# Retention's gate as seven half-size products between the value blocks, and the first head's projection between retention's steps

## The chip, the cores and the metric

The kernel runs on one core of a Trainium2 chip. Its engines run side by side, each with an instruction stream of its own, and wait for each other through semaphores: TensorE (PE) multiplies into the PSUM banks, VectorE (DVE) and ScalarE (ACT) take the results out and prepare operands, GpSimd (POOL) does small elementwise work, and SP, ACT and POOL issue the DMAs. An engine takes its instructions strictly in order; what stands behind a waiting instruction waits with it. The metric is the device time of one execution in microseconds (us): the median of the runs before is 1484.71 us, from 1483.43 to 1484.89.

## What is computed

One step of a decoder layer for a prompt of 1024 tokens and 8 single decode tokens: a mixer (differential attention beside retention), attention into a memory, and an MLP. The change concerns the input projection of the mixer and retention. Cut to that:

```python
z = rmsnorm(x) @ w_in                    # 1024 features in
qa, ka, va, qr, kr, vr, gr = split(z)    # va, vr and gr: 512 columns each
# retention, 4 heads, chunks of 128 tokens (C)
scores = (q @ k.T) * decay
o      = scores @ v + (q @ S) * exp((i + 1) * lg)
S      = exp(C * lg) * S + k_dec.T @ v
r      = head_rms(o) * silu(gr)          # gr is the gate
x      = x + concat(a, r) @ w_out        # a: attention, from qa, ka, va
```

Matrix products run in a reduced-precision fp32 form. So each operand is split into a high part and a low rest (names ending in h and l, or UH/UL and wh/wl), and a product takes three matmuls: high by high, high by low, low by high.

## The kernel before

Five stretches follow each other on TensorE at the front of the kernel, and the change touches all but the first.

1. **Projection of retention's q and k** for all tokens, while x is loaded.
2. **Value block "va"** and **value block "vr"**, both by `token_block` (L478). A block computes a projection of 512 columns for 1024 tokens as seven products of half-size matrices in place of eight (a Strassen-like scheme: the right operands are quadrants of the weights or their sums, the left ones quadrants of x or their sums in `XT`). The seven products come in the order 1, 2, 6, 7, 4, 5, 3, with 48 matmuls of 256 columns each, 336 in all, and 32 more with few rows for the decode tokens. Their results are added up by ACT and DVE in the tiles `va` or `vr`, in SBUF (L530 to L540). `between` hangs work of the other engines between the products: `after_va` writes the finished va rows to DRAM by DMAs that ACT issues (L594), rotates some q/k rows (`rotate`, on POOL and DVE) and makes bias rows; `after_vr` rotates the others and fetches and splits the gate's weights.
3. **Retention's 8 steps** (loop over `t`), one per 128 tokens. A step transposes q and k (`tr`, to `qblk` on ACT and `kT` on DVE), multiplies the scores `sc`, masks them into `Sm` (DVE), forms the state's increment `st` and the output `op` from `Sm`, v and the running state `S`. Between these short pieces stands the gate's projection for the same 128 tokens as filler, `grp` (`tokproj_parts`, L405): 24 matmuls of 512 columns per step, dealt out by `SEG = (3, 4, 0)` groups of three. At t = 2 come 16 more matmuls for the decode tokens' gate. The end of a step is `head_norm_gate`: squares of `op` on ACT (`jk`), a small scaling on DVE (`s4`), a power on POOL (`r4`), and the multiplication by the gate on DVE. One step later `to_operand` transposes the result (`trR`), splits it (`rh` on ACT, `rl` on DVE), and POOL issues two DMAs that write it to DRAM (`OPH`, `OPL`).
4. **Attention's first head**: `head_proj(0)`, 144 matmuls of 344 columns named `qkp`. The first 36 and then as many as complete two thirds of it, 96 in all, run as a block; then come 36 more (`START`) while `load_part` splits the keys (`KA`, `KB`), which POOL's DMAs copy into place on other partitions.
5. **Attention's score loop**, beginning with the matmuls `sp<-KA,Q`, whose gaps the rest of the projections fills.

The order on each engine is written out in the code: a `pin` keeps the matmuls in program order, `behind(...)` puts instructions after the last one of another engine, and the rest follows the order of the code by a scheduler. The number of buffers of a tile (`bufs`) sets when its next use may begin.

Of the kernel before, what the change touches and what calls it, by code (L numbers as in the profile page):

```python
# [10 lines left out]
F32 = mybir.dt.float32  # L11
# [3 lines left out]
ALU = mybir.AluOpType  # L15
# [33 lines left out]
def decoder_step(ctx: ExitStack, tc: tile.TileContext, i: dict, o: dict):  # L49
# [113 lines left out]
    ord_ = dram.tile([4, 8, P], F32, tag="ord", name="ord_")  # L163

# [17 lines left out]
    t_front, v_front = ExitStack(), ExitStack()  # L182
# [203 lines left out]
    with pool("a") as A:  # L386
# [6 lines left out]
        def decproj(units, name, PS, out, bufs=3):  # L393

            ps = PS.tile([P, 512], F32, tag="acc", name=name, bufs=bufs)

            dproj(ps, units)
            merge_parts(ps, out, name)
            return out

# [3 lines left out]

        def tokproj_parts(units, t, name, PS):  # L405
            ps = PS.tile([P, 512], F32, tag="acc", name=name, bufs=3)
            tk = slice(t * P, t * P + P)
            for kt in KT_PAIRS:
                w = [u[:, (kt // 4) * 512 : (kt // 4) * 512 + 512] for u in units[kt % 4]]
                mm(ps, UH[:, kt, tk], w[0], kt == 0, False)  # L410
                mm(ps, UH[:, kt, tk], w[1], False, False)
                mm(ps, UL[:, kt, tk], w[0], False, kt == 7)
                yield ps
# [64 lines left out]
        def token_block(ready, nm, out_dec, fetch, between, after):  # L478
# [12 lines left out]
            def scale(t):  # L491
                if t > 3 and nm == "vr":
                    return
                y = acc[t // 2][:, t % 2, :]
                cs = slice(256, 512) if t < 4 else slice(0, 512)
                nc.scalar.activation(y[:, cs], y[:, cs], AF.Copy, scale=rstd1[:, t : t + 1])

            order = (1, 2, 6, 7, 4, 5, 3)
            for n, q in enumerate(order):
# [13 lines left out]
                for pb in range(2):  # L513
# [14 lines left out]
                    with behind("Activation", "DVE"):  # L528
                        if q == 1:
                            nc.scalar.copy(lo[:, :, b], pv)  # L530
                        elif q == 2:
                            for j in range(2):
                                nc.scalar.activation(lo[:, j, a], pv[:, j, :], AF.Copy, scale=rstd1[:, 2 * pb + j : 2 * pb + j + 1])
# [7 lines left out]
                if q in (1, 2, 4, 5):  # L541
# [6 lines left out]
                    if q == 5:  # L548
                        merge_parts(psd, out_dec, nm)
                        nc.scalar.activation(out_dec, out_dec, AF.Copy, scale=rstd1[:8, 8:9])  # L550
# [35 lines left out]
        rot_va, rot_vr = {4: 8, 5: 0, 3: 1}, {1: 2, 2: 3, 6: 4, 7: 5, 4: 6, 5: 7}  # L586

        def after_va(q, acc):
# [8 lines left out]
            if q in rot_va:  # L597
                rotate(rot_va[q])

        def after_vr(q, acc):  # L600
            if q in rot_vr:
                rotate(rot_vr[q])
            if q == 5:
                nc.scalar.dma_start(vrd, vr8[:8])
                nc.scalar.activation(silu, half, AF.Silu)
            if q in (5, 3):
                for u in range(2):
                    if q == 3:
                        late = G.tile([P, T], F32, tag="raw", name="raw_g1", bufs=3) if u else G.tile([P, T], F32, tag="rb2", name="raw_g0")
                        nc.sync.dma_start(late[:, :1024], i["wall"][U_TOK + 10 + u])  # L610
                        late_raws.append(late)
                    else:
                        units.append(unit(U_TOK + 8 + u))
# [12 lines left out]
        units, late_raws = [], []  # L626
        pin[0] = True
        op_vr = token_operands(U_TOK + 4, "vr")
        token_block(op_va, "va", vdec[:8], rot_va, after_va, op_vr)
        vr8 = A.tile([P, 512], F32, tag="t1", name="vr_8", bufs=1)  # L630
        vacc = token_block(op_vr, "vr", vr8[:8], rot_vr, after_vr, lambda q: None)
# [3 lines left out]
        t_front.close()  # L635
        r_front = ExitStack()
        A = r_front.enter_context(pool("r", side="right"))
# [14 lines left out]
        def head_norm_gate(src, gate, n, t, out):  # L652
# [3 lines left out]
            for h in range(4):  # L656
                jk = A.tile([P, P], F32, tag="jk", name=f"jk_{t}_{h}")
# [8 lines left out]
        def to_operand(src, n, t, tag, tags=("rh", "rl", 1)):  # L666

            tr = PS.tile([P, 512], F32, tag="tr", name=f"trR_{tag}", bufs=tags[2])
# [13 lines left out]
        gate_d = A.tile([8, 512], F32, tag="gate_d", name="gate_d")  # L682

        tr = PS.tile([P, 512], F32, tag="acc", name="tr_d", bufs=3)
# [6 lines left out]
        def decode_step(p):  # L691
            so = raw_tile(A, f"so_{p}")
# [21 lines left out]

        S = None
        uqk = {}
        pend = None
        pin[0] = True
        for t in range(8):
            tr = PS.tile([P, 512], F32, tag="tr", name=f"tr_{t}", bufs=1)  # L720
# [8 lines left out]
            if t == 6:  # L729
                with behind("DVE"):  # L730
                    next(scaled)
            grp = tokproj_parts(units, t, f"grp_{t}", PS)
            for _ in range(SEG[0]):
                next(grp)
# [3 lines left out]
            Sm = A.tile([P, 512], F32, tag="Sm", name=f"Sm_{t}", bufs=2)  # L738
            nc.vector.tensor_mul(Sm, sc, maskM)
            if t == 0:  # L740
                with behind("Activation", "DVE"):
                    units += [unit(U_TOK + 10 + u, raw=late_raws[u]) for u in range(2)]
# [4 lines left out]
            if pend:  # L747
                pend()
            for _ in range(SEG[1]):
                next(grp)  # L750
            if t == 3:
                with behind("SP"):
                    nc.sync.dma_start(brep, bass.AP(tensor=brow[:, :].tensor, offset=brow[:, :].offset, ap=[[0, P], [1, 4 * BIASW]]))
            if t == 7:
                uqk[0] = [unit(U_QK + x) for x in range(2)]
# [13 lines left out]
            S = Sn  # L769
# [1927 lines left out]
```

## Time and profile before

One execution was profiled. Its own time is 1483.49 us, 1.2 us below the median of the runs.

| what | value |
|---|---|
| time of the profiled execution | 1483.49 us |
| span of its instructions | 1481.7 us |
| granted TensorE clock, mean | 0.997 of full |
| ACT busy, share of the span | 46% |
| POOL busy, share of the span | 21% |
| DMA, mean over the span | 160 GB/s |

The page gives for each engine the time in which an instruction ran and its share of the span. Matmuls overlap each other in their pipeline, so the duration of one (say 0.28 us) is longer than the distance at which the next one starts (0.118 us); distances between starts give the cost of a matmul in a row of them. Rows of a group or a tile show a count, durations (least, median, most, or the mean) and when the first and the last one started. Rows of waits show who waited for whom, in total, how often, and the longest wait.

### The profile page before, as it was taken

The numbers are of one execution on the slowest core, as the hardware profiler recorded it, in microseconds if no ns is written. First come the engines' busy times: TensorE is split into PE (matmuls) and PEld (weight loads), VectorE is DVE, ScalarE is ACT, GpSimd is POOL, SyncE is SP. The second block draws the span as 40 slices with busy tenths as digits, with TensorE's granted clock in tenths as the row PEclk, the third lists the DMA queues.
The fourth block names the chain that finished last, engine by engine and source line by source line (L and its number), as shares of the span: only waits on it lengthen the run. The fifth ranks groups of instructions, "written<-read, shape, count | busy, mean of one in ns | idle before, by whom it ended". The sixth has DMA issues, their size and how long they took to land.

```text
span 1481.7 us, 27906 instructions
## 1 busy us (share of the span) xinstructions
PE 1468.0 (99%) x10917; PEld 1399.2 (94%) x10917; DVE 1097.3 (74%) x2265; ACT 677.6 (46%) x1328; POOL 305.6 (21%) x331
## 2 busy tenths in 40 slices
PE   9999999999999999999999999999999999999998
PEld 7899779999679999989999999999999999999998
DVE  7666536888768545567877987888888888787876
ACT  6534435666552341258536544333434443343454
POOL 0035333122214311106022000000001311110380
PEclk9999999999999999999999999999999999999998
DMA  8255738214846177474582443334446774536273
GB/s 288 68 187 169 205 70 190 72 34 143 253 145 242 68 247 189 118 237 109 179 299 69 157 148 131 141 137 157 158 144 211 239 252 143 172 102 194 79 130 115
DMA packets 125784, 236.69 MB, mean 160 GB/s; under 512 B 13654, under 2 KB 75787, under 8 KB 125524
## 3 DMA queue, kind: packets, MB, share of 16 engines
q1 hardware_dynamic: 90826, 174.52, 37.2%
q0 software_dynamic: 23632, 40.60, 10.2%
q10 hardware_dynamic: 11194, 19.78, 3.6%
q8 instruction: 86, 1.41, 0.4%
q14 instruction: 46, 0.38, 0.1%
HBM read 170.24 MB, written 57.52 MB: 154 GB/s over the span
## 4 chain that ended last, share of the span: by engine, by line
PE 90%; DVE 5%; ACT 2%; issue 1%; DMA 1%; ACTq 0%; POOL 0%; SPq 0%; DVEq 0%
PE dn L2345 21%; PE Z L2177 9%; PE qkp L75 7%; PE pr_o L75 6%; PE mq L75 6%; PE pr_m L75 6%; PE X L2177 6%; PE Y L2177 6%; PE grp L75 3%; PE sp L75 2%; PE av L75 2%; PE mv L75 2%; PE mk L75 1%; PE mpv L75 1%; PE vap_z L522 1%
## 5 line engine op out<-in xcount | busy, mean ns | idle before, releaser
L2345 PE MATMUL dn<-UH,wd 128*128 128x258 f32 (+1 forms) x1800 | 325.9, 283 | 0.9 <-DVE c L2479 0.8
L2345 PEld LDWEIGHTS dn<-UH,wd 128*128 128x128 f32 x1800 | 278.7, 189 | 1.8 <-DVE c L2479 0.8
L2345 PE MATMUL dn<-UL,wd 128*128 128x258 f32 x900 | 253.9, 282 | 0.0
L2345 PEld LDWEIGHTS dn<-UL,wd 128*128 128x128 f32 x900 | 169.7, 189 | 0.1
L2479 DVE TENSOR_TENSOR c<-c,dn 128x258 f32<-128x258 f32 (+1 forms) x217 | 88.8, 417 | 36.7 <-PE dn L2345 34.2
L2203 ACT ACTIVATE hq<-r 128x258 f32<-128x258 f32 x128 | 53.7, 421 | 118.0 <-DVE r L2202 117.9
L2177 PE MATMUL Z<-T_h,wu 128*128 128x258 f32 x512 | 98.1, 283 | 0.0
L2177 PE MATMUL X<-UH,wu 128*128 128x258 f32 x512 | 97.5, 282 | 0.0
L2321 ACT CAST wd<-raw_d 128x512 fp32r<-128x512 f32 x96 | 58.7, 619 | 79.6 <-PE dn L2345 74.1
L1985 ACT CAST wu<-raw_up 128x512 fp32r<-128x512 f32 x96 | 59.0, 616 | 61.0 <-PE Z L2177 53.2
L2314 ACT CAST UH<-raw_h 128x1032 fp32r<-128x1032 f32 x56 | 58.7, 1055 | 53.3 <-PE dn L2345 27.7
L2177 PEld LDWEIGHTS X<-UH,wu 128*128 128x128 f32 x512 | 81.3, 188 | 0.0
L2177 PEld LDWEIGHTS Z<-T_h,wu 128*128 128x128 f32 x512 | 81.3, 189 | 0.0
L2315 DVE TENSOR_TENSOR UL<-raw_h,UH 128x1032 fp32r<-128x1032 f32 x56 | 73.7, 1315 | 8.4 <-ACT UH L2314 8.4
L2322 DVE TENSOR_TENSOR wd<-raw_d,wd 128x512 fp32r<-128x512 f32 x96 | 72.2, 758 | 10.3 <-ACT wd L2321 10.3
L2214 POOL DMA_DIRECT2D HT<-ht x32 | 17.1, 536 | 292.0 <-DVE ht L2213 271.6
L2177 PE MATMUL Z<-T_l,wu 128*128 128x258 f32 x256 | 72.3, 282 | 0.0
L2177 PE MATMUL X<-UL,wu 128*128 128x258 f32 x256 | 72.3, 282 | 0.0
L128 ACT CAST wh_u<-raw_u 128x1024 fp32r<-128x1024 f32 x43 | 44.5, 1048 | 57.3 <-PE mq L75 36.4
L1986 DVE TENSOR_TENSOR wu<-raw_up,wu 128x512 fp32r<-128x512 f32 x96 | 64.8, 689 | 3.7 <-ACT wu L1985 3.7
L129 DVE TENSOR_TENSOR wl_u<-raw_u,wh_u 128x1024 fp32r<-128x1024 f32 x39 | 48.6, 1257 | 19.8 <-ACT wh_u L128 19.6
L75 PE MATMUL qkp<-UH,wh_u 128*128 128x344 f32 x192 | 62.8, 327 | 0.1
(606 smaller groups left out, 4657.2 us busy)
## 6 DMA issues: line engine op xcount, KB each, us to landing
raw_u<-in_wall SPq DMA_DIRECT2D x49, 512.0 KB
HT<-ht POOLq DMA_DIRECT2D x32, 516.0 KB, 3.0
raw_h<-HT SPq DMA_DIRECT2D x32, 516.0 KB
raw_up<-in_wall SPq DMA_DIRECT2D x32, 512.0 KB
raw_d<-in_wall SPq DMA_DIRECT2D x32, 512.0 KB
HQ<-hq ACTq DMA_DIRECT2D x32, 387.0 KB
raw_h<-HQ SPq DMA_DIRECT2D x24, 516.0 KB
cmk<-in_cmk SPq DMA_DIRECT2D x16, 512.0 KB
```

Source lines behind the costliest of these rows:

```text
L75: pinned(nc.tensor.matmul(out, l, r, start=start, stop=stop))
L129: (lo_engine or nc.vector).tensor_sub(wl[:, :n], raw[:, :n], wh[:, :n].bitcast(F32))
L1985: nc.scalar.copy(w[:, :512], src)
L1986: nc.vector.tensor_sub(w[:, 512:], src, w[:, :512].bitcast(F32))
L2177: pinned(nc.tensor.matmul(ps, l, r[:, k, :], start=first and k == 0 and x == 0, stop=k == 3 and x == 2, skip_group_check=True))
L2203: nc.scalar.activation(h[:, PLACE[quad], :], r, AF.Square)
L2314: nc.scalar.copy(h, rv)
L2315: nc.vector.tensor_sub(l, rv, h.bitcast(F32))
L2321: nc.scalar.copy(w[:, :512], src)
L2322: nc.vector.tensor_sub(w[:, 512:], src, w[:, :512].bitcast(F32))
L2345: pinned(nc.tensor.matmul(ps[:, part], l, r[:, k, cq], start=first and k == 0 and x == 0, stop=k == 3 and x == 2, skip_group_check=True))
L2479: nc.vector.tensor_add(y, y, ps)
```

## The change

- **The gate becomes a third block "ga"** of `token_block` between "va" and "vr", with Silu as the function that takes the results out of PSUM. `grp`, its 16 decode matmuls and `SEG` are gone. The gate's weights are laid out like those of the values.
- **The gate's rows go through DRAM.** ACT issues eight DMAs of 256 KB and a small one into the new tensor `gated`; retention's steps fetch their rows back on SP's queue (`fetch_gate`).
- **Work between the products moves.** The rotations of `after_vr` move to `after_ga`; the load of the Silu table and a one-column Silu, which stood in the vr block's product 5, move to the end of va. The 2304 KB copy `brep`, from retention's step 3, is issued in the vr block's product 1; `rb`, a broadcast row that attention needs, in its product 3; the split of head 0's weights (`head_units(0)`) in its product 5.
- **`head_proj(0)` fills retention's steps**, by `RFILL = (8, 6, 5)`: 8 matmuls ahead of the loop, then 6 between `st` and `op` and 5 after `op`, 96 in all. The transposes of the next step (`turn_step`) move between `st` and `op`, the multiplication by the gate moves into the next step, `trR` comes after `op`, and head 1's weights are split in step 5.
- **After the loop** come `load_stacks` and `load_part` at once, 30 matmuls of filler, the last `to_operand`, and 6 more (`START = 6`).
- **Buffers**: `acc` banks 3 to 2, `tr` 1 to 2, `Sm` 2 to 1, the gate's tiles 2 to 3.

The core of the diff:

```diff
-        def tokproj_parts(units, t, name, PS):
-            ps = PS.tile([P, 512], F32, tag="acc", name=name, bufs=3)
...
+            if q == 3:
+                nc.scalar.activation(silu, half, AF.Silu)
+
+        def after_ga(q, acc):
+            if q in rot_ga:
+                rotate(rot_ga[q])
+            for t in {5: range(4), 3: range(4, 8)}.get(q, ()):
+                nc.scalar.dma_start(gated[t * P : t * P + P, :], acc[t // 2][:, t % 2, :])
+            if q == 5:
+                nc.scalar.dma_start(gated[NT:, :], ga8[:8])
 
         def after_vr(q, acc):
-            if q in rot_vr:
-                rotate(rot_vr[q])
+            if q == 1:
+                nc.sync.dma_start(brep, bass.AP(tensor=brow[:, :].tensor, offset=brow[:, :].offset, ap=[[0, P], [1, 4 * BIASW]]))
             if q == 5:
                 nc.scalar.dma_start(vrd, vr8[:8])
-                nc.scalar.activation(silu, half, AF.Silu)
...
+                head_units(0)
+            if q == 3:
+                nc.gpsimd.dma_start(rb, bcast_rows(rrow[0:1, :], P, T))
...
+        op_ga, op_vr = token_operands(U_TOK + 8, "ga"), token_operands(U_TOK + 4, "vr")
+        token_block(op_va, "va", vdec[:8], rot_va, after_va, op_ga)
+        token_block(op_ga, "ga", ga8[:8], rot_ga, after_ga, op_vr, AF.Silu)
+        vacc = token_block(op_vr, "vr", vr8[:8], {}, after_vr, lambda q: None)
...
+        fill(RFILL[0])
+        for t in range(8):
+            qb, kT = turned
...
+            Sm = A.tile([P, 512], F32, tag="Sm", name=f"Sm_{t}", bufs=1)
...
+            if t < 7:
+                turned = turn_step(t + 1)
+            if scaled:
+                with behind("DVE"):
+                    next(scaled)
+            fill(RFILL[1])
...
+            if pend:
+                pend()
+            fill(RFILL[2])
+            scaled = head_norm_gate(op, gate, P, t, gate)
+            next(scaled)
+            pend = lambda gate=gate, t=t: to_operand(gate, P, t, f"{t}", ("rh", "rl", 1))
+            if t < 7:
+                gate = fetch_gate(t + 1)
...
+            if t == 5:
+                with behind("Activation", "DVE"):
+                    head_units(1)
...
-        fill(36)
-        to_operand(gate, P, 7, "7", ("ah", "al", 2))
-        until(0, 1, 0)
-        with behind("Activation", "DVE"):
-            head_units(1)
         load_stacks(0)
         for _ in load_part(0, EARLY):
             pass
         filler = chain(filler, rest())
+        fill(30)
+        to_operand(gate, P, 7, "7", ("ah", "al", 2))
...
-START = 36
+START = 6
...
-SEG = (3, 4, 0)
+RFILL = (8, 6, 5)
```

**ACT at the end of va.** This is ACT's order where va ends and the next block's first results (`x` bank, product 1) are copied out. Before:

```order
L496 ACTIVATE va_700<-va_700,rstd_87 128x512 x2
L496 ACTIVATE va_701<-va_701,rstd_87 128x512 x2
L594 DMA out_v_p<-va_700 128x512 x2
L594 DMA out_v_p<-va_701 128x512 x2
L530 COPY vr_1066<-vrp_x_1070 128x2x256
L530 COPY vr_1067<-vrp_x_1096 128x2x256
L128 CAST wh_vr_1137<-raw_vr_903 128x1024
```

Of the change:

```order
L479 ACTIVATE va_701<-va_701,rstd_88 128x512 x2
L479 ACTIVATE va_702<-va_702,rstd_88 128x512 x2
L577 DMA out_v_p<-va_701 128x512 x2
L577 DMA out_v_p<-va_702 128x512 x2
L583 ACT_TABLE_LOAD
L583 ACTIVATE silu<-half 128x1
L513 COPY ga_1068<-gap_x_1072 128x2x256
L513 COPY ga_1069<-gap_x_1098 128x2x256
L128 CAST wh_ga_1139<-raw_ga_904 128x1024
```

The table load and the small Silu now stand between the DMAs of va's rows and the copies for which the next block's product 2 waits.

**DVE in retention.** This is DVE's order from one step's `kT` to the next one's, with the mask multiplication `Sm`, the state `S` and the multiplication by the gate (`gate<-op,r,gate`). Before, step 4 (`kT` of step 4 to `kT` of step 5):

```order
L728 COPY kT_1969<-tr_1962 128x256
L663 SCALAR_TENSOR_TENSOR gate_1942<-op_1923,r_3_1945,gate_1942 128x128 x4
L739 TENSOR_TENSOR Sm_1984<-sc_1981,maskM 128x512
L768 SCALAR_TENSOR_TENSOR S_2023<-S_1932,rdec,st_1986 128x128 x2
L674 TENSOR_TENSOR rl_1997<-trR_1991,rh_1996 128x512
L139 TENSOR_SCALAR s_4_2031<-s_4_2031 128x4
L728 COPY kT_2054<-tr_2047 128x256
```

Of the change, from step 3's `Sm` to step 4's `Sm`:

```order
L785 TENSOR_TENSOR Sm_2274<-sc_2271,maskM 128x512
L808 SCALAR_TENSOR_TENSOR S_2309<-S_2237,rdec,st_2276 128x128
L145 SCALAR_TENSOR_TENSOR UL<-xagain_2022,g_mix,UH 128x512 x2
L760 COPY kT_2288<-tr_2281 128x256
L697 SCALAR_TENSOR_TENSOR gate_2185<-op_2228,r_2_2257,gate_2185 128x128 x4
L808 SCALAR_TENSOR_TENSOR S_2309<-S_2237,rdec,st_2276 128x128
L642 SCALAR_TENSOR_TENSOR qraw_2055<-qkp_0_0_2147,rb 128x344
L708 TENSOR_TENSOR rl_2318<-trR_2312,rh_2317 128x512
L139 TENSOR_SCALAR s_3_2330<-s_3_2330 128x4
L740 SCALAR_TENSOR_TENSOR sn_2341<-so_2193,rdec,vb_2195 128x512 x2
L785 TENSOR_TENSOR Sm_2349<-sc_2346,maskM 128x512
```

The gate of step 2 (`gate_2185`, which `trR` of step 2 transposes behind step 3's `op`) is now multiplied in step 3, behind the restoring of x's low part (`UL<-xagain`); the results of the filler (`qraw`) and the decode tokens' state (`sn`) stand ahead of step 4's `Sm`.

**POOL ahead of the first keys.** This is POOL's order from the last steps of retention to the first copies of head 0's keys. Before:

```order
L676 DMA OPH<-rh_d 128x4x8
L140 TENSOR_TENSOR r_7_2328<-s_7_2327,half 128x4
L676 DMA OPL<-rl_d 128x4x8
L1048 MEMSET ah_0_0_2701 128x128
L676 DMA OPH<-rh_2425 128x4x128
L1048 MEMSET al_0_0_2702 128x128
L676 DMA OPL<-rl_2426 128x4x128
L992 TENSOR_TENSOR VL_2746<-vraw_2570,VH_2745 128x512 x2
L965 DMA KA_0_2511<-KA_0_2511 64x688
L967 DMA KB_0_2513<-KB_0_2513 64x688
```

Of the change:

```order
L710 DMA OPH<-rh_2623 128x4x128
L710 DMA OPL<-rl_2624 128x4x128
L140 TENSOR_TENSOR r_7_2636<-s_7_2635,half 128x4
L710 DMA OPH<-rh_d 128x4x8
L710 DMA OPL<-rl_d 128x4x8
L965 DMA KA_0_2684<-KA_0_2684 64x688
L967 DMA KB_0_2686<-KB_0_2686 64x688
L965 DMA KA_0_2685<-KA_0_2685 64x688
L967 DMA KB_0_2687<-KB_0_2687 64x688
```

The copies of the keys now stand right behind the decode tokens' operand (`rh_d`, `rl_d`) and step 6's (`rh_2623`, `rl_2624`); step 7's comes after them.

220 lines of the change are left out of this document (89 added, 131 removed).

## The prediction

> **What bounds the kernel now.** I read the page's busy times first.
>
> ```profile
> PE 1468.0 (99%) x10917; PEld 1399.2 (94%) x10917; DVE 1097.3 (74%) x2265; ACT 677.6 (46%) x1328; POOL 305.6 (21%) x331
> ```
>
> TensorE is busy for 99% of the span, so the time falls only by matmul work taken away, and it rises wherever the change makes TensorE wait. Next I read the starts of the matmuls, which give the price of the pieces. First the value block that the new gate block copies (rows of the tiles' matmuls with count, durations, first and last start; then the chain of waits; then TensorE's waits from 45 to 145 us).
>
> ```profile
> L522 PE MATMUL vrp_x<-wh_vr,UH x32: 276/281/387, 99.7 to 112.5; 128*128 128x256 f32 x32
> ```
> ```profile
> 144.33 0.34 PE tr_d L686 x4
> ```
> ```profile
> PE vrp_x L522 <- ACT vr L530: 0.6, 1, 0.6
> ```
>
> The vr block runs from 99.7 to 144.3, where `tr_d` begins: 44.6 us, with one wait of 0.6 for ACT. A block without waits is **44.0 us**, for 336 + 32 matmuls, or 0.12 each. Now retention, in step 4 (timeline of TensorE: start, duration).
>
> ```profile
> 190.15 1.13 PE L75 MATMUL sc<-qblk,kT 128*128 128x256 f32 x4
> 191.21 0.66 PE L75 MATMUL st<-vr,qk 128*64 128x128 f32 x8
> 191.80 0.66 PE L78 MATMUL trR<-ident,gate 128*128 128x128 f32 x4
> 192.21 0.48 PE L75 MATMUL grp<-wh_u,UH 128*128 128x512 f32 x1
> ...
> 195.08 0.38 PE L75 MATMUL op<-vr,Sm 128*128 128x128 f32 x2
> ...
> 196.78 0.48 PE L75 MATMUL grp<-wh_u,UH 128*128 128x512 f32 x1
> ...
> 200.16 0.92 PE L75 MATMUL sc<-qblk,kT 128*128 128x256 f32 x3
> ```
>
> A step takes 200.16 − 190.15 = 10.01 us. Twelve `grp` matmuls lie between 192.21 and 195.08, 0.239 each; 24 of them are 5.74, so the step's own products are 10.01 − 5.74 = **4.27** (sc 1.06, st 0.59, trR 0.41, op 1.70, the rest tr). Last, the end of the stretch.
>
> ```profile
> 248.79 0.32 PE L75 MATMUL qkp<-UH,wh_u 128*128 128x344 f32 x1
> ...
> 250.67 0.28 PE L75 MATMUL sp<-KA,Q 128*128 128x256 f32 x1
> ```
>
> Twelve `qkp` matmuls take 250.67 − 248.79 = 1.88, or 0.157 each; the first scores start at 250.67. From `tr_d` to there TensorE needs 250.67 − 144.33 = **106.3 us** now. Since the same 132 filler matmuls (36 + 60 + 36 before, 96 + 30 + 6 of the change) lie in it, everything later has the same work left.
>
> **The change part by part.** *The gate block* adds 44.0.
>
> *The same stretch without waits.* At its start come tr_d 0.34, a tr of about 0.4 (what is left of the step's own work), and 8 fillers of 0.157: 2.0. Eight steps of 4.27 + 11 × 0.157 = 6.00 are 48.0. Less trR and half of op in step 0 (0.41 + 0.85) and a tr in step 7 (0.4): −1.6. Step 5 has the decode product besides:
>
> ```profile
> L75 PE MATMUL opd<-vb,hsel x8: 592/604/617, 207.7 to 208.1; 128*32 128x512 f32 x8
> ```
>
> which takes about 1.0 (208.1 + 0.6 − 207.7). Then 36 fillers (5.65), trR (0.41) and the decode operand's transposes (estimated at 0.2): 6.3. Together 2.0 + 48.0 − 1.6 + 1.0 + 6.3 = 55.7, so 106.3 − 55.7 = 50.6 go and 44.0 come: **−6.6**. That is the change if nothing waits. Every step is 4 us shorter, though, and the other engines' work in it is not; this cover is what I now price.
>
> *Boundary va to ga.* The vr block's wait of 0.6 stays here: ACT, held up by va's rows, copies the first results late. The chain of waits shows it, and the table load's rows show what is put in front of that copy.
>
> ```profile
> 97.68 2.34 ACTq L594
> ```
> ```profile
> L605 ACT ACT_TABLE_LOAD  x1: 1283/1283/1283, 140.7 to 140.7; - x1
> L605 ACT ACTIVATE silu<-half x1: 204/204/204, 142.0 to 142.0; 128x1 f32<-128x1 f32 x1
> ```
>
> ACT is already the late one here, so load and Silu, 1.28 + 0.20, pass to TensorE in full: +1.5 (0 if ACT had time by then, 1.5 at most). In the old place product 3's matmuls hid them. [...] The boundary ga to vr repeats va's pattern of four DMAs on ACT: 0 to 0.6 by the wait of 0.6, I take 0.3. *Gate rows*: eight DMAs issued on ACT stand beside the products, and the fetches on SP come a step or more ahead; 0, unless the case of `brep` below holds.
>
> *Chains in the short steps.* Rows of DVE, ACT and POOL from 144 us on (busy in all, mean ns of one):
>
> ```profile
> L663 DVE SCALAR_TENSOR_TENSOR gate<-op,r,gate 128x128 f32<-128x128 f32 x28 | 7.9, 344 | 3.8 <-POOL r L140 3.8
> L739 DVE TENSOR_TENSOR Sm<-sc,maskM 128x512 f32<-128x512 f32 x8 | 5.5, 684 | 3.4 <-PE sc L75 3.4
> ...
> L705 DVE SCALAR_TENSOR_TENSOR sn<-so,rdec,vb 128x512 f32<-128x512 f32 x4 | 3.0, 746 | 0.0
> L145 DVE SCALAR_TENSOR_TENSOR UL<-xagain,g_mix,UH 128x512 fp32r<-128x512 f32 x4 | 2.8, 748 | 1.4 <-ACT UH L144 1.4
> ```
> ```profile
> L658 ACT ACTIVATE jk<-op 128x128 f32<-128x128 f32 x32 | 8.9, 278 | 22.6 <-PE op L75 22.2
> L658 ACT ACTIVATION_READ_ACCUMULATOR jk<-op 128x1 f32 x32 | 6.4, 200 | 0.0
> ```
> ```profile
> L140 POOL TENSOR_TENSOR r<-s,half 128x4 f32<-128x4 f32 x8 | 8.2, 1024 | 29.9 <-DVE s L139 25.3 <-DMA vb<-vrd 4.6
> L676 POOL DMA_DIRECT2D OPH<-rh x8 | 6.4, 794 | 18.5 <-ACT rh L673 18.5
> ```
>
> And one piece of the later chain of waits, the split of head 1's weights:
>
> ```profile
> 261.24 1.14 DVE wl_u L129
> ```
>
> From the end of op to its trR one step on, TensorE has 6.0 us (a step of 6.00). In that time come four squares with reads (4 × 0.48 = 1.9), scaling and power (1.2) and four gate products (4 × 0.34 = 1.4, less by overlap): 4.5. Alone that fits, with 1.5 to spare. In steps 1 and 3 the gate product stands on DVE behind the two UL (1.5) and what they wait for on ACT: about 1.1 late each. Between sc and op, TensorE has st, tr and 6 fillers, about 1.9; Sm needs 0.7. Where it stands behind two sn (steps 2 and 4, 1.5) it is about 0.3 late, behind two wl_u (step 6, 2.3) about 1.5. In step 5 the filler's next PSUM bank, of which there are now two and opd takes one, waits for ACT's copy and the `kraw` product: about 1.0. Sum 1.1 + 0.3 + 1.1 + 0.3 + 1.0 + 1.5 = 5.3. Bounds: 0, if the engines use the idle time that the same rows show (ACT 22.6, POOL 29.9 over the steps), and 9, if none of the five waits shortens the next. I take **5.0**, since a wait gives the next chain some time.
>
> *First scores.* Before, the keys' copies were issued 7 us ahead of their use (rows of the tile KA; landings of OPH's DMAs, of KA's over 230 to 270 us, of KA's over the whole run).
>
> ```profile
> L964 ACT CAST KA<-kraw x4: 467/618/768, 242.0 to 251.0; 64x688 fp32r<-64x688 f32 x2, 64x336 fp32r<-64x336 f32 x2
> L966 DVE TENSOR_TENSOR KB<-kraw,KA x4: 501/689/1040, 242.8 to 251.7; 64x688 fp32r<-64x688 f32 x2, 64x336 fp32r<-64x336 f32 x2
> L965 POOL DMA_DIRECT2D KA<-KA x4: 515/520/577, 243.1 to 252.3; - x4
> ```
> ```profile
> DMA to landing us min/median/max: 2.9/2.9/10.9
> ```
> ```profile
> DMA to landing us min/median/max: 5.0/5.5/5.8
> ```
> ```profile
> DMA to landing us min/median/max: 2.3/5.1/9.3
> ```
>
> In the change TensorE reaches the scores 6.3 us after step 7's last filler. By then rh of step 6 is just written; ACT's rh_d, which has the same single buffer, waits for OPH of step 6 to land (0.8 + 2.9), then come the two KA casts and the KB rest on DVE (0.8 + 1.0) and POOL's issues (0.5 each): KB leaves about 6.0 us after that filler and lands 2.3 to 5.8 later, at 8.3 to 11.8. TensorE waits 2.0 to 5.5; I take **3.6**. [...]
>
> *Given back.* Head 1's weights are split in step 5 already, so the piece of 1.14 at 261.24 goes from the later chain: −1.2 (0, if something else is late there, to −2, with ACT's part of the split).
>
> **Sum**, against the profiled execution's 1483.5: −6.6 + 1.5 + 0.3 + 5.0 + 3.6 − 1.2 = **+2.6**, 1486.1. The median of the runs is 1.2 above that execution, so I forecast 1487.3, rounded to **1487**.
>
> **The rivals.** *The steps hide it (faster).* If ACT's and POOL's idle time suffices and the keys land like the least row, what stays is −6.6 + 1.5 + 0.3 + 1.0 + 1.5 − 1.2 = −3.5, and −5 without the boundary: 1479.7 to 1481.2. For it speaks that the bare chains fit (4.5 in 6.0, and 0.7 in 1.9) and only what stands ahead of them on DVE makes them late; against it, that three engines and the keys' landing must all be on time, step after step.
>
> *`brep` holds the gate's rows (slower).* SP issues brep as soon as the last rotation row is fetched, some 15 us before the ga block's end, and ACT's third DMA of the second half of the gate's rows takes the completion counter that, as I count the counters in their order, brep had. ACT's instruction then waits for brep, and behind it stand the copies that the vr block's product 2 needs, about 19 us after brep's issue. Before, brep left at 150.1:
>
> ```profile
> L753 SPq DMA_DIRECT2D brep<-brow x1: 1484/1484/1484, 150.1 to 150.1; - x1
> ```
> ```profile
> 155.00:165.00 10.00, 9.97 (x61) 7.99 (x61) 4.76 (x12) 3.61 (x15) 4.51 (x4) 1.00 1.08 337
> ```
>
> The window's DMA share (next to last column) is full up to 165, so brep took about 15 us. It decides from 19 us on; each us beyond is one lost. With the weights of the vr block ahead of it, 22 to 24 us, 3 to 5 lost: 1490 to 1492.
>
> *The saving isn't there.* If a 256-column matmul cost half of a 512-column one plus a fixed share, the seven products would save nothing; but 0.12 against 0.239 is a half, so I give it no chance of its own.
>
> **How the numbers follow.** 0.2% is 3 us, about what a measurement of this kernel tells from no change. The forecast's case, exposed chains that eat the saving, has 0.62, from 1481.7 to 1490; of it 0.40 lie within 0.2% (up to 1487.7) and 0.22 above. The hidden case has 0.22, all faster; brep 0.16, all slower. So faster 0.22, same 0.40, slower 0.38. The range takes 1480 to 1492: it leaves out the best of the hidden case and the worst of brep and of the chains.
>
> **What would show it.** Right: in the changed profile a row of waits of the first scores for KA or KB of 2 to 5 us; the ga block's product 2 waiting about 2 us for ACT's copy behind the table load; steps of 6 to 7.5 us, with waits of op for Sm in step 6 and of trR for the gate in steps 1 and 3; `grp` gone and 336 matmuls of `gap` 0.12 us apart. Wrong: steps of 6.0 throughout, or a vr block that waits for ACT's DMA for several us. The forecast falls most easily by the keys' landing and by the steps' chains, since both were worked out in a row from single durations.

## The result, and the profile after

The changed kernel takes 1493.21 us (median of 4 runs, 1491.05 to 1495.38) against 1484.53 us (1483.43 to 1484.89) of the kernel before on the same chip: the ratio is 1.0060, with a 95% interval of 1.0042 to 1.0077. It is about **8.7 us slower**; the forecast was 2.6 us slower, with a range that ended at 1492.

The profiled execution took 1491.05 us, with a span of 1489.1 us, 7.4 us more than before. The page's busy times of the kernel after:

```profile
PE 1465.3 (98%) x11077; PEld 1405.8 (94%) x11077; DVE 1113.9 (75%) x2282; ACT 681.0 (46%) x1337; POOL 304.6 (20%) x331
```

TensorE is busy 2.7 us less than before (1468.0), in a span 7.4 us longer: matmul work went, and more waiting came. The tile rows show that the two large terms of the sum were real (first and last start stand behind the durations):

```profile
L505 PE MATMUL gap_x<-wh_ga,UH x32: 277/280/385, 99.1 to 111.9; 128*128 128x256 f32 x32
```
```profile
L505 PE MATMUL vrp_x<-wh_vr,UH x32: 277/281/388, 143.6 to 156.7; 128*128 128x256 f32 x32
```
```profile
L75 PE MATMUL sc<-qblk,kT x32: 377/379/455, 190.8 to 235.1; 128*128 128x256 f32 x32
```

The gate block runs from 99.1 to 143.6, 44.5 with a wait of 0.6 for ACT (below), so it costs 43.9 without waits (forecast 44.0). The scores of retention's eight steps lie between 190.8 and 235.1; step 7's begin some 0.8 before the last of them, so a step takes (235.1 - 0.8 - 190.8) / 7 = 6.2 us, with the decode product in one of the seven. It was 10.0. The saving is there. TensorE's waits from 45 to 320 us (total, times, longest) show what came with it:

```profile
PE sp L75 <- DVE mn L1016: 2.5, 2, 1.8
PE trR L78 <- DVE rl_d L708: 1.9, 1, 1.9
PE vrp_x L505 <- ACT vr L513: 0.9, 1, 0.9
PE op L75 <- DVE Sm L785: 0.8, 1, 0.8
PE sp L75 <- DMA KA<-KA: 0.8, 1, 0.8
PE sp L75 <- DMA KB<-KB: 0.8, 1, 0.8
PE gap_x L505 <- ACT ga L513: 0.6, 1, 0.6
PE trA L78 <- DVE e L1031: 0.4, 1, 0.4
PE sc L75 <- DVE kT L760: 0.2, 1, 0.2
```

That is 8.9 us. Before, the same view had three rows, 1.6 us together. Inside retention only 1.0 of it lies (`op` and `sc`); 6.4 lie at its end and behind it. TensorE's timeline at that place:

```profile
245.82 0.31 PE L75 MATMUL qkp<-UL,wh_u 128*128 128x344 f32 x1
245.97 0.32 PE L75 MATMUL qkp<-UH,wl_u 128*128 128x344 f32 x1
248.18 1.11 PE L78 MATMUL trR<-ident,gate 128*128 128x128 f32 x4 [1.88 <-DVE rl_d L708]
...
249.66 0.49 PE L75 MATMUL qkp<-UH,wl_u 128*128 128x344 f32 x1
249.95 0.49 PE L75 MATMUL qkp<-UH,wh_u 128*128 128x344 f32 x1
...
251.78 0.36 PE L75 MATMUL sp<-KA,Q 128*128 128x256 f32 x1 [0.77 <-DMA KA<-KA]
252.90 0.39 PE L75 MATMUL sp<-KB,Q 128*128 128x256 f32 x1 [0.76 <-DMA KB<-KB]
```

Two things are to be seen. TensorE idles ahead of step 7's `trR`. And the filler behind that wait is slow: the matmuls start 0.29 us apart, where ahead of it they start 0.15 to 0.16 apart. The windows of after (start:end, length, busy time of PE, PEld, DVE, ACT and POOL with the instructions in brackets, then the granted clock, the DMA share and GB/s) say why:

```profile
244.00:248.00 4.00, 2.29 (x14) 1.81 (x12) 1.10 (x5) 2.47 (x5) 0.78 (x1) 1.00 0.88 170
248.00:252.00 4.00, 3.05 (x11) 2.58 (x11) 3.89 (x6) 1.80 (x3) 3.58 (x7) 0.57 0.60 97
252.00:256.00 4.00, 3.24 (x22) 3.11 (x22) 3.53 (x9) 1.92 (x5) 1.70 (x3) 1.00 0.57 198
```

The clock is 0.57 in the second window: a stretch of (1 - 0.57) x 4 / 0.5 = 3.4 us at half of full speed. Before, every window from 240 to 256 has 1.00. And DVE, which was nearly idle while TensorE waited (1.10 of 4 us), is full from then on (3.89 of 4). Its rows, and POOL's:

```profile
247.93 0.19 DVE L708 TENSOR_TENSOR rl_d<-trR_d,rh_d 128x32 fp32r<-128x32 f32 x1 [2.90 <-ACT Q L972]
248.21 1.76 DVE L966 TENSOR_TENSOR KB<-kraw,KA 64x688 fp32r<-64x688 f32 x2
250.00 3.45 DVE L973 TENSOR_TENSOR Q<-qraw,Q 64x688 fp32r<-64x688 f32 x2
...
258.80 1.37 DVE L1165 COPY rel<-relb 32x32 f32<-32x32 f32 x1
```
```profile
242.08 0.75 POOL L710 DMA_DIRECT2D OPL<-rl  x1 [0.81 <-DVE rl L708]
...
249.16 0.56 POOL L965 DMA_DIRECT2D KA<-KA  x1
...
251.39 1.32 POOL L992 TENSOR_TENSOR VL<-vraw,VH 128x512 fp32r<-128x512 f32 x1
...
258.79 1.34 POOL L992 TENSOR_TENSOR VL<-vraw,VH 128x512 fp32r<-128x512 f32 x1
```

DVE stands at `rl_d`, the low part of the decode tokens' operand, for 2.90 us. The view names an instruction of ACT as releaser, but the row of POOL tells what it was: `rl_d` has the single buffer of step 6's `rl`, whose DMA `OPL`, issued at 242.08, had to land first (5.8 us). Behind `rl_d` stand KB and Q; `trR` of step 7 stands behind it for its PSUM bank. So the keys' DMAs leave at 249.16. In the kernel before, `rl_d` was written and KA had gone (243.1) when TensorE still had 7 us of filler. And two of DVE's instructions are stretched: Q's pair takes 3.45 where the kernel before has 1.77, `rel` 1.37, each while POOL runs VL. Before:

```profile
248.04 1.77 DVE L973 TENSOR_TENSOR Q<-qraw,Q 64x688 fp32r<-64x688 f32 x2
```

The starts of the same matmuls in both traces (after less before, each from its own first instruction) give the course of the loss: +1.1 at the first scores, +5.2 only 12 us later (at 263.5 of before), then slowly up to +7.4.

### The profile page after: what moved, and what is told of

It is laid out like the page before. It is cut to its first block, busy times and chain, and to the rows that moved or that the text cites. A ratio compares the mean times of both kernels' runs of the same rounds, so it can differ in the third digit from the quotient of the medians.

```text
span 1489.1 us, 28346 instructions
## 1 busy us (share of the span) xinstructions
PE 1465.3 (98%) x11077; PEld 1405.8 (94%) x11077; DVE 1113.9 (75%) x2282; ACT 681.0 (46%) x1337; POOL 304.6 (20%) x331
## 2 busy tenths in 40 slices
DMA packets 128266, 241.45 MB, mean 162 GB/s; under 512 B 13943, under 2 KB 76076, under 8 KB 128005
## 4 chain that ended last, share of the span: by engine, by line
PE 82%; DVE 7%; DMA 6%; ACT 2%; issue 2%; POOL 1%; ACTq 0%; DVEq 0%; SPq 0%; POOLq 0%
PE dn L2334 19%; PE Z L2166 9%; PE qkp L75 7%; PE pr_m L75 6%; PE X L2166 6%; PE Y L2166 6%; PE mq L75 5%; PE pr_o L75 4%; PE sp L75 2%; PE av L75 2%; PE mpv L75 1%; PE vap_z L505 1%; PE gap_z L505 1%; PE vrp_z L505 1%; DMA raw_h<-HQ 1%
## 5 line engine op out<-in xcount | busy, mean ns | idle before, releaser
L75 PE MATMUL qkp<-UH,wl_u 128*128 128x344 f32 x192 | 63.1, 328 | 0.0
```

The lines of the kernel that those rows point to most:

```text
L75: pinned(nc.tensor.matmul(out, l, r, start=start, stop=stop))
```

## The experiments

My theory after the traces was: TensorE is made to wait at the end of retention by the single buffer of `rl`; then the half clock and a DVE that has everything at once make it late behind that. Rivals: the table load; the loss is work missing as filler there; nothing but the keys' DMAs counts. All ratios are to the kernel before, on the same chip, whose median beside these runs lay between 1482.0 and 1483.2.

| kernel | edits | median us | ratio, 95% interval |
|---|---|---|---|
| after | | 1493.21 | 1.0060, 1.0042 to 1.0077 |
| e1 | own buffers | 1488.61 | 1.0048, 1.0029 to 1.0067 |
| e2 | START 30 | 1494.47 | 1.0085, 1.0069 to 1.0102 |
| e3 | own buffers, START 30 | 1490.81 | 1.0060, 1.0043 to 1.0077 |
| e4 | table load earlier | 1490.74 | 1.0055, 1.0038 to 1.0072 |
| e5 | idle matmuls | 1491.59 | 1.0055, 1.0042 to 1.0068 |
| e6 | own buffers, idle matmuls | 1488.80 | 1.0042, 1.0029 to 1.0055 |
| e7 | own buffers, head 2 by DMA | 1487.85 | 1.0031, 1.0020 to 1.0042 |
| e8 | own buffers, table load earlier | 1487.32 | 1.0026, 1.0016 to 1.0036 |
| f1 | own buffers, head 2 by DMA, table load earlier | 1486.08 | 1.0021, 1.0012 to 1.0030 |
| f2 | f1, keys first | 1490.63 | 1.0055, 1.0041 to 1.0069 |
| f3 | f2, VL on DVE | 1491.01 | 1.0051, 1.0038 to 1.0064 |
| f4 | f1, VL on DVE | 1485.18 | 1.0023, 1.0013 to 1.0032 |
| f5 | f4, idle matmuls | 1484.25 | 1.0011, 1.0001 to 1.0021 |
| f6 | f4, START 20 | 1485.88 | 1.0023, 1.0012 to 1.0035 |
| f7 | f4, START 12 | 1483.43 | 1.0009, 1.0000 to 1.0018 |

**e1: the decode operand in buffers of its own** (those of `kT`, 256 columns wide, idle by then).

```diff
-        to_operand(gate_d, 8, 8, "d")
+        to_operand(gate_d, 8, 8, "d", ("kT", "kT", 2))
```

> The changed kernel, but the decode tokens' operand (rh_d, rl_d) gets buffers of its own (kT's, free by then), so that rl_d no longer waits on DVE for OPL of step 6 to land. Theory 1 (this one wait holds DVE, and with it KB, Q and the first score masks): the trR wait of 1.9 goes, the waits of the first scores for KA, KB and mn fall from 4.0 to under 2, time 3 to 4 us below the changed kernel, about 1489 to 1490. Theory 2 (casts, POOL's issues and the landing of the keys are themselves too long for the 6 us before the scores): KA and KB still leave late, at most 1 us gained, 1492 to 1493.

The row of `trR` for `rl_d` is gone, and no window from 240 to 260 has a clock below 1.00. TensorE's waits of e1:

```profile
PE sp L75 <- DMA KA<-KA: 1.8, 1, 1.8
PE sp L75 <- DVE mn L1016: 1.7, 1, 1.7
```

In its profiled execution the first scores start 1.9 us earlier than in the kernel before, and the span (1482.3) is 6.8 below after's. Behind the first scores it loses 1.6 us (from 1.9 ahead to 0.3 ahead), where after lost 4.1. The median gains 0.0012, within the intervals: part of e1's runs had a mean clock of 0.995 to 0.996 and took 1490.7 to 1491.6, the others 0.998 and 1484.6 to 1486.5. The single buffer is a cause in the trace, but not the whole; for the time, e4 against e8 below decides.

**e2 and e3: more filler ahead of the first scores**, alone and with e1's buffers.

```diff
-START = 6
+START = 30
```

> The changed kernel with START = 30: 24 more filler matmuls (3.8 us) ahead of the first scores, and as many fewer behind. Theory 1 and theory 2 alike: the waits for KA, KB and mn (4.0 us) vanish, the trR wait (1.9) stays, 3 to 4 us gained, about 1489 to 1490. Rival 3 (the loss after the first scores is no wait for the keys but a lack of filler): the gain comes back as waits at the end of the projections, no change, 1493.

> Both edits. Theory 1: no wait is left before the score loop, 5 to 6 us gained, 1487 to 1488. Theory 2: as START = 30 alone.

Filler does not heal it. In e2 the wait for KA is gone, but that of `trR` stays (2.1), the scores wait 3.2 for `mn` and the kernel is the slowest of all. In e3 the keys are on time and the scores wait 3.9 us for `mn`: the first scores stand 0.3 us behind those of the kernel before, and 12 us later the same matmuls 3.8. So behind the first scores **DVE** is late, whatever the keys do. Its rows, POOL's and TensorE's of e3 show by what:

```profile
252.78 3.80 DVE L129 TENSOR_TENSOR wl_u<-raw_u,wh_u 128x1024 fp32r<-128x1024 f32 x1
```
```profile
252.93 2.55 POOL L992 TENSOR_TENSOR VL<-vraw,VH 128x512 fp32r<-128x512 f32 x2
```
```profile
256.84 0.38 PE L75 MATMUL sp<-KA,Q 128*128 128x256 f32 x1 [2.14 <-DVE mn L1016]
```

One `wl_u`, a piece of the split of head 2's weights, takes 3.80 us instead of 1.22 while POOL runs VL, and the masks behind it come late. 2.3 of the 3.5 us lost behind e3's first scores stand there. The rest comes at a second wait for `mn`, of 1.8.

**e4: the Silu table's load earlier**, in va's product 2, the second of the seven, instead of behind the last (at 70 us instead of 104).

```diff
             if q == 2:
                 split_sums(1)
+                nc.scalar.activation(silu, half, AF.Silu)
...
-            if q == 3:
-                nc.scalar.activation(silu, half, AF.Silu)
```

> The changed kernel with the load of the Silu table and the small Silu in va's product 2 instead of at va's end. The prediction's term (load and Silu pass to TensorE in full): 1.5 us gained, 1491.7. Rival (ACT had room: the wait at ga's product 2 is 0.6 as it was at vr's before): 0 to 0.6 gained.

The wait of `gap_x` for ACT (0.6) is gone from e4's rows, the ratio moves by 0.0005, within the intervals. By these two traces the load was worth about half of a microsecond and not 1.5. That price is not fixed: in e7's execution below, with the load at va's end, `gap_x` waits 1.4 for ACT.

**e5: TensorE kept busy in its waits**: 12 matmuls of 344 columns ahead of step 7's `trR`, 10 ahead of the first scores, whose result nothing uses.

```diff
+        for _ in range(12):
+            mm(busy[:, :CH], UH[:, 0, 0:P], UH[:, 0, 0:CH], True, True)
         to_operand(gate, P, 7, "7", ("ah", "al", 2))
```

> The changed kernel with 22 matmuls of 344 columns added whose results nobody reads: 12 (1.9 us) ahead of the trR of step 7, 10 (1.6 us) ahead of the first scores, where TensorE waits 1.9 and 1.5 us in the changed kernel. They shorten no wait; they keep TensorE busy in it. Theory 4 (an idle TensorE of about 2 us is followed by some 3.5 us at a granted clock of 0.5, which costs as much again, and in most executions this happens more than once): no window below 1.00 between 240 and 260, the mean clock back to 0.997 or 0.998 in all executions, and 2 to 5 us less than the changed kernel, which stood 8.7 us above the one before. Rival (the clock has nothing to do with it): same time or up to 1 us more.

A window of e5 at the place where after has the half clock:

```profile
240.00:250.00 10.00, 9.36 (x58) 8.57 (x58) 4.95 (x16) 4.79 (x12) 4.55 (x6) 1.00 0.65 122
```

The clock stays at 1.00 and the mean of every run at 0.997 to 0.998 (after: 0.993 to 0.997); the runs now lie between 1490.09 and 1492.78. So it was the idling that lowered the clock at this place. But the median hardly moves: the same waits for `mn`, `e` and the keys (1.5, 1.1, 1.2) follow on a fast TensorE. **e6**, e1 with 12 such matmuls ahead of the first scores, says the same:

> Buffers of its own for the decode tokens' operand, and 12 matmuls of 344 columns (1.9 us) whose results nobody reads ahead of the first scores, where that kernel still waits 1.8 us for KA. Theory 4: its slow executions (up to 1491.6 beside a kernel before of 1482.0) were ones in which the clock fell after this wait; they go, and the median comes to 2 to 3 us above the kernel before. Rival: as with own buffers alone, 6.6 above.

It is 0.0006 below e1, within both intervals, and its profiled execution has a half-clock stretch elsewhere, at 780 us.

**e7: DVE relieved.** Head 2's low weights, which DVE splits behind the first scores, by ACT and a DMA that adds up (the kernel has a function for it); with e1's buffers. **e8**: e1 with e4.

```diff
-            uqk[h] = [unit(U_QK + 2 * h + x) for x in range(2)]
+            uqk[h] = [(unit_by_dma if h == 2 else unit)(U_QK + 2 * h + x) for x in range(2)]
```

> Buffers of its own for the decode tokens' operand, and the low parts of head 2's weights by ACT and a DMA that adds, instead of by DVE (two times 1.2 us off DVE among the first scores). Theory 3 (behind retention DVE is the bound: what TensorE gains upstream it waits for there, in waits of the scores for mn): these waits fall from 1.7 to under 1, 1 to 2 us gained over own buffers alone (6.6 above the kernel before). Rival (mn waits by POOL's contention or the keys alone): no gain.

> Buffers of its own for the decode tokens' operand, and the load of the Silu table in va's product 2. If the load at va's end costs in some executions only (then with a wait at ga's product 2 and a fallen clock behind it), the spread of 7 us goes and the median falls 2 to 3 us below own buffers alone, to 4 above the kernel before; if it costs nothing, 6.6 above.

In e7 two splits of 1.14 us moved from DVE to ACT and a DMA and nothing else. The scores' wait for `mn` (1.7 in e1) is gone, the keys' wait (1.8) stayed, and a new one for DVE stands behind the scores:

```profile
PE trA L78 <- DVE e L1031: 1.0, 1, 1.0
```

So DVE is late there, but less of it is won than the 1.7 suggest: behind the first scores e7's execution loses 1.1 us, e1's 1.6. The ratio is 0.0017 below e1's, with intervals that overlap. e8 is 0.0022 below e1, more than e4's 0.0005 leads to expect, and why is not shown; in its profiled execution `wl_u` took 3.65 us beside POOL's VL, against 1.14. The clear comparison is e8 with e4, which differ by the decode operand's buffers alone: 1.0026 against 1.0055, with intervals apart. By these two the single buffer costs about 0.003, half of the change's loss.

**f1: the three together. f2: the keys first**, by moving the decode operand behind step 7's. **f3: VL of head 0 on DVE** in f2.

```diff
-        to_operand(gate_d, 8, 8, "d", ("kT", "kT", 2))
...
         to_operand(gate, P, 7, "7", ("ah", "al", 2))
+        to_operand(gate_d, 8, 8, "d", ("ah", "al", 2))
...
-                eng = nc.vector if h == 3 and cs.start == 0 else nc.gpsimd
+                eng = nc.vector if h == 0 or (h == 3 and cs.start == 0) else nc.gpsimd
```

> The three edits that each helped a little, together: the decode operand in buffers of its own, head 2's low weights by ACT and a DMA that adds up instead of by DVE, the Silu table loaded in va's product 2. If their gains add (ratio to the kernel before 1.0048 for the first alone, 1.0031 with the second, 1.0026 with the third in place of the second, 1.006 for the change itself), about 1.001, that is +0.5 to +2.5 us, with no fall of the granted clock between 240 and 280 us and no wait of trR for rl_d. If head 2's weights and the table load only remove the same slack, which the next late chain takes up, 1.0025 to 1.003, as each alone.

> f1 with the decode tokens' operand (trR_d, rh_d, rl_d and POOL's two DMAs of it) moved behind step 7's, so that the keys' DMAs stand directly behind step 6's operand on POOL. Theory that the distance of the keys' copies to their use is a cost of its own: KA and KB leave about 1.5 us earlier, the scores' wait for KA falls from about 1.8 to under 0.5, and the time by 1 to 1.5 us against f1. Rival that DVE's backlog sets the pace behind the first scores whatever the keys do: the wait for KA goes and the one for mn or trA's wait for e grows by as much, the time within 0.5 us of f1.

> f2 with the low half of head 0's values (VL, two instructions) on DVE instead of POOL, where each ran 1.3 us at a time beside DVE. Theory that DVE is slowed while POOL runs VL (Q 2.55 in place of 0.87, a 32x32 copy 1.3 in place of 0.15, wl_u 3.65 in place of 1.14): VL costs DVE 1.4 us of its own and saves 1.5 to 2.5 us of such stretching, so DVE's longest of Q, rel and wl_u come back to 0.9, 0.2 and 1.2 and the time falls by 0 to 1 us. Rival that DVE's time for these is due to something else (their input's arrival): they stay long and the time rises by up to 1.4 us.

f1 is between its two forecasts, and the half clock came back in its profiled execution (0.50 from 250 to 252). f2 is a miss: with the decode operand gone, a small copy of `kraw` on ACT (`kdec`) came to stand ahead of the casts of KA. It waited 4.8 us for a product of DVE that stands behind step 7's gate products, so KA left at 247.0 instead of 244.5, and its two DMAs landed after 7.7 us instead of 5.0 (medians). What made the landing longer I did not test. f2's wait and its windows, with TensorE's busy time first:

```profile
PE sp L75 <- DMA KA<-KA: 6.1, 1, 6.1
```
```profile
250.00:252.00 2.00, 0.00 (x0) 0.00 (x0) 1.51 (x4) 1.95 (x5) 1.43 (x2) 1.00 0.93 305
252.00:254.00 2.00, 0.00 (x0) 0.00 (x0) 0.00 (x0) 1.98 (x2) 1.56 (x3) 0.78 1.81 228
254.00:256.00 2.00, 1.09 (x3) 0.82 (x4) 0.00 (x0) 0.18 (x1) 0.56 (x2) 0.50 2.15 225
256.00:258.00 2.00, 2.00 (x9) 2.00 (x8) 1.21 (x6) 0.49 (x2) 1.53 (x3) 0.50 2.43 267
258.00:260.00 2.00, 2.00 (x10) 2.00 (x9) 0.48 (x3) 0.60 (x2) 1.45 (x4) 0.51 1.51 231
```

It does not tell the value of an earlier issue, but it shows the clock once more: a wait of 6 us, then half clock from about 253 to 260, some 6.8 us by these windows, 5.1 us of it with TensorE busy.

**f4: f1 with VL on DVE. f5: f4 with 14 idle matmuls** ahead of the first scores. **f6 and f7: f4 with START = 20 and 12**, so that real work stands there instead.

> f1 with the low half of head 0's values (VL) on DVE, two instructions of about 0.69 us, instead of on POOL, two of 1.3, in whose time DVE's copy rel took 2.87 in place of 0.15. Theory that this stretching delays the masks e and so the scores: rel takes 0.15 to 0.3, DVE has 2.7 - 1.4 = 1.3 us less to do between 248 and 262, and the time falls by 0.5 to 1.5 us against f1 (ratio 1.0011 to 1.0018). Rival that DVE has slack there in f1: no change, 1.0018 to 1.0026; and that VL's 1.4 us stand ahead of the first masks: up to 1 us more.

> f4 with 14 idle matmuls of 344 columns (2.2 us, their result is used by nothing) in TensorE's wait ahead of the first scores, where f1 idled 2.15 us and then ran for about 3.3 us with matmuls 0.285 instead of 0.157 us apart. If the half clock there costs what the distances say, 3.3 x (1 - 0.157/0.285) = 1.5 us, the clock stays at 1.00 from 240 to 280 us, the fastest runs move little and the slower ones come down: median 0.5 to 1.5 us below f4. Rival that DVE sets the pace of the scores behind it and hides a slower TensorE: no change against f4 within 0.5 us, or up to 0.5 more for the idle matmuls that outlast the wait.

> f4 with START = 20 instead of 6, so that 14 matmuls of the next projection (14 x 0.157 = 2.2 us) fill TensorE's wait for the first keys, where f5 had idle ones. Theory that behind the first scores TensorE, not DVE, is now late (f5's only wait of scores there is 1.1 us for mn): the 2.2 us of work are done for nothing, the clock stays at 1.00, the scores' wait for KA falls to under 0.5 and the time lies 1 to 2 us below f5, ratio 0.9997 to 1.0005. Rival that the scores' masks on DVE set the pace and the 14 matmuls are missing as filler: the wait for mn grows from 1.1 to 3 us and the ratio stays at 1.0009 to 1.0025.

> f4 with START = 12: six matmuls more, 0.95 us of the wait. By the first theory half of f6's gain over f4 (KA's wait 1.0, the time 0.5 to 1.2 us below f4, 1.0012 to 1.002, with the clock saved if an idle of about 1 us does not lower it); by the rival as f4, 1.002 to 1.003.

DVE's row of `rel` in f1, POOL's beside it, and DVE's in f4:

```profile
252.11 2.87 DVE L1163 COPY rel<-relb 32x32 f32<-32x32 f32 x1
```
```profile
252.38 2.55 POOL L990 TENSOR_TENSOR VL<-vraw,VH 128x512 fp32r<-128x512 f32 x2
```
```profile
252.62 0.38 DVE L1163 COPY rel<-relb 32x32 f32<-32x32 f32 x1
```

With VL off POOL the stretching is gone (in f3 too: its two `rel` take 0.25 together), but f4's ratio is that of f1: DVE had room for it there, as the rival had it. Both have head 2's splits off DVE, so what the stretching costs with `wl_u` in its way, as in e3, was not tested. Keeping TensorE busy does count now: f5 is 0.0012 below f4, ten of its 11 runs lie below ten of f4's 12, and these ten have a clock of 0.997 to 0.998. f5's first scores start 2.7 us earlier than those of the kernel before, and 12 us later it is still 1.9 ahead. f6's 14 real matmuls in the same place bring nothing. That they lack as filler behind fits its wait of 2.2 us for `mn` (f5's: 1.1), but no run shows it apart. Six more (f7) give 1.0009, better than was expected of them and not to be told from f5. Its profiled execution was its slowest run, 1488.80 us, with a late landing of KB and half clock behind it:

```profile
PE sp L75 <- DMA KB<-KB: 3.2, 1, 3.2
```
```profile
254.00:256.00 2.00, 2.00 (x9) 2.00 (x8) 1.61 (x4) 0.33 (x3) 1.56 (x4) 0.50 1.32 282
```

No version beats the kernel before. f5 and f7 are within 0.2% of it, and both are clearly faster than the change as it was made.

## Why the prediction was wrong

The direction was right and the time outside the range. Measured terms are those of the profiled execution, whose span grew by 7.4.

| step of the sum | predicted | measured | from |
|---|---|---|---|
| ahead of the gate block | 0 | -0.6 | the va block begins at 54.21, before at 54.80 |
| gate block and shorter stretch | -6.6 | -6.9 | 43.9 for each of the two blocks, before 44.0 for the one; 55.7 (the sum's, what exceeds it is below) for 106.4 |
| boundaries | +1.5, +0.3 | +0.9 | waits 0.6 + 0.9, before 0.6 |
| chains in the steps | +5.0 | +2.3 | `tr_d` to the end of step 7's last filler 51.7, 49.4 by the same sum without waits |
| decode operand and the 30 fillers | in -6.6 | +1.2 | 240.03 to 246.13, 6.1 for 4.9 by the sum |
| first scores | +3.6 | +4.3 | 248.18 and 251.78 against 245.97, below |
| behind the first scores | -1.2 | +4.1 | +1.1 to +5.2 |
| later | 0 | +2.2 | +5.2 to +7.4 |

The first six rows add up to +1.2, against +1.1 measured at the first scores. The decode operand's transposes, estimated at 0.2, took 1.1 with their waits for DVE's `gate_d`.

- **The step that failed is "Given back".** It took the piece of 1.14 (`wl_u`, at 261.24 before) for head 1's split. It is head 2's, and it is still there after the change (at 266.3, and another at 256.7). The sum ended at the first scores and let everything behind them be as before, so a loss of 4.1 us had no term. What the runs show in its place: with the keys late, DVE has KB, Q, the masks `e` and two `wl_u` to do in one heap, two instructions in it (a Q and `rel`) are stretched beside VL, by 2.9 us in all, and the scores wait for it. Of the 4.1, 1.0 is lost between the first KA and KB matmuls, at KB's landing and at half clock; 0.9 and 1.0 at the two waits for `mn`; the rest in smaller pieces. e1, with DVE let go in time, loses 1.6 there. e3 shows DVE late with the keys on time (3.5), most of it behind the one stretched `wl_u`; e7 shows that 2.3 us less of DVE work take the wait for `mn` away and leave one of 1.0 for `e`. How the 4.1 divide between the heap and the stretching stays open.
- **The half clock had no term either.** The prediction knew only the mean of 0.997. From 246.13, where the filler ends, to the first scores at 251.78 are 5.65 us, of which `trR` and six fillers need 0.41 + 0.94 at full clock. Of the 4.3 that are left the waits take 2.05 + 0.77, so about 1.5 is the half clock. The other three runs may have had more of it: one stretch like that of the profiled run would by estimate lower a run's mean clock by 3.4 x 0.5 / 1489 = 0.0011 and cost 1.7 us, and they lie at 0.993 to 0.995 and 1.7 to 4.3 us above the profiled one (0.997); no trace of them shows where. The lowest clock does not go with the longest time, so this explains a part of the spread and not each run.
- **First scores: the mechanism in kind, not in place.** The reuse of a single buffer behind a landing was foreseen, for `rh_d` on ACT, which OPH lets go. What came last was `rl_d` on DVE, behind OPL, issued 1.6 us later, with a landing of 5.8 where 2.9 was taken (`rh_d` did wait for OPH, 4.7 us); and it held `trR` too, which the prediction had not seen queued there. The waits alone are 2.8, smaller than 3.6, and the half clock brings the sum above it. The first rival's 1.5 for this place is shown by no run: the least landing gives 8.3 - 6.3 = 2.0, and the first scores came 4.3 late. e1 takes the cause away.
- **Chains in the steps: mis-sized**, 5.0 for 2.3. Of the rows announced only `op` for `Sm` came (0.8); `trR` never waited for the gate in steps 1 and 3. ACT's and POOL's idle time did hide them, as the first rival had it. Half of that rival was right, which the failed step more than ate. The upper bound of 9 had no rows behind it.
- **Table load: about 0.5** (e4, uncertain by its interval) for 1.5. The premise was that ACT is late at this boundary. But before, ACT's three DMA issues of va's first rows took 3.26 us, one of them 2.34; in the profiled execution after the change the same three took 1.35, so the load stood in time that had come free. In e7's execution the wait was 1.4, as forecast. What sets the length of the issues is not shown.
- **`brep` holds the gate's rows: refuted in its size.** It was issued at 135.2 and had landed at 149.3. In after's trace ACT's third DMA of the second half does wait for `brep`'s counter (semaphore 105); it went at 149.4, where ACT's issue before it ended at 148.6, so this cost 0.7 us at most. Of the gate's DMAs on ACT one took 2.1 us, at 146.5, the copies behind them waited 2.9 at most, and TensorE's `vrp_x` 0.9.
- **Open: the last 2.2 us**, and the like growth of f5 (from -1.9 to +0.9). They come in pieces of 0.4 to 0.9 where TensorE waits for DVE or ACT far behind the change (`dop`, `mv`, `dn`), and in f5 some 1.4 us by a fall of the clock between 760 and 800 us (0.96 over that window, before 1.00). No run separates the change's part of it from the spread of the runs.

## What to carry to other kernels

When work is taken out of a stretch, follow every engine's queue to the place where the next stage starts, and add up what the others have still to do there: the covered work does not vanish, it heaps up behind the first instruction that is late. Ask of each single-buffered tile in such a place which DMA must have landed before it is written again. Look also at what runs beside it: an instruction that is stretched there is late work too (`rel` took 2.87 us for 0.15 in f1, beside POOL's VL). And where TensorE waits for about 2 us, look at the clock behind the wait: it was 0.50 for 3.4 us behind 1.9 in after, and 1.00 behind 1.9 in f4.

## What the hardware showed that was not expected

- **Half clock after waits of about 2 us, and not every time.** TensorE waited 1.9 us in after (2.05 from the end of the matmuls before), 2.1 in e2 and 2.2 in f1, and a stretch at half speed followed, of 3.4 us in after; it waited 1.8 in e1 and e7, 1.9 in f4 and 2.1 in e3, and none followed. Nor did every such stretch stand behind a long wait. In e6 the clock is 0.50 from 781 to 782 us and 0.83 over the window from 780 to 790, right behind 16 matmuls of 8 columns and this one short wait among them. The kernel before has the same matmuls and the same wait, without the half clock:

```profile
777.75 0.75 PE L75 MATMUL pr_m<-UH,wh_u 128*128 128x258 f32 x4 [0.26 <-ACT UH L2098]
```
```profile
781.00:782.00 1.00, 1.00 (x6) 1.00 (x6) 1.00 (x1) 0.00 (x0) 0.00 (x0) 0.50 0.08 16
```

  What decides between the two cases is not shown: a wait of 1.9 us stands on both sides.
- **DVE instructions were stretched beside POOL's VL.** In f1 `rel`, 0.15 us, took 2.87 while POOL ran two VL (2.55); in f4, with VL on DVE, it took 0.38. In e3 a `wl_u` took 3.80 for 1.22. Not every DVE instruction was: before, POOL ran its two VL from 240.56 to 243.10, and `kraw`, which reads a PSUM bank, took its usual 0.52 beside them at 241.45. DVE had little else to do then; the change moved VL behind the keys' DMAs, into DVE's fullest time.
